# Moving the operands of every matmul to multiples of 128 and 1024 bytes in their partition

## The chip, the cores and the metric

The kernel runs on one core of a Trainium2 chip. The metric is the device time of one execution in microseconds (us), as the median of the runs. Five engines take part: TensorE (PE in the profile; its loads of stationary tiles are PEld), VectorE (DVE), ScalarE (ACT), GpSimd (POOL) and SyncE (SP), which here only issues DMAs.

## The reference

One decoder layer on x of 256 tokens by 1024 features, all in float32:

```python
h = rmsnorm(x, g_pre)
q_a, k_a, v_a, g_a, x_m, z_m = split(h @ w_in)      # w_in: 1024 x 6144
o_a = causal attention, 8 heads of 128, plus a bias by distance
y_a = o_a * silu(g_a)
x_c = silu(depthwise conv of width 4 over x_m)
q_m, k_m, v_m = block-diagonal 4x4 projections of x_c, x_c, x_m
h_m = mLSTM (4 heads of 256) with gates from q_m, k_m, v_m, then a LayerNorm per head
y_m = (h_m + skip * x_c) * silu(z_m)
out = x + rmsnorm(concat(y_a, y_m) @ w_out, g_post)  # w_out: 2048 x 1024
```

## The kernel before, in words

**Precision and tiles.** The two large projections use the type fp32r. Each float32 operand is split into a hi part, rounded to fp32r, and a lo part, the rest; a product is hi*hi + hi*lo + lo*hi, so three matmuls stand for one. The input projection goes through 24 chunks of 256 columns of `w_in` (8 tiles of 128 rows by 256 columns, a `raw` tile of 1 MB); the output projection goes through 8 chunks of `w_out`, 1 MB each. SyncE's queue brings the chunks four ahead (L76), ScalarE rounds them into `hi` (L90) and VectorE subtracts to get `lo` (L100). There are three buffers each of raw, hi and lo.

**The input projection.** `hhi` and `hlo` hold the transposed input, scaled by `g_pre`, 8 tiles of 128x256. `project` (L512) handles half a chunk in one call: 24 matmuls with 256 moving columns, stationary a 128x128 piece of the weights and moving a piece of `hhi` or `hlo`; for the v chunks stationary and moving change places. The first two chunks go through `project_quarter` (L522), quarter by quarter as the data comes in.

**The order.** It is written out by hand (manual schedule). The list `chunks` says which chunk is next: four of x_m ("m"), four of the gate g, then q, k and v of each pair of attention heads, the z chunks before the last pair. Two slots make a chunk. After each chunk `evacuate` scales its PSUM bank and starts a generator (`conv`, `gates`, `mlstm_head`, `attend`, `gate_a`, `gate_z`); in each slot `run_side` issues the next step of every generator that is due ahead of the half chunk's matmuls. Small matmuls thus stand between the halves: `vps` (L279) and `qps` (L286) of the block-diagonal projections, `gp` (L297) and `gif` (L304) of the gates, transposes `cp` (L331), `ht` (L389) and `atp` (L426) with `ident`, scores `sp` (L341, L344) and `as` (L406, L407), and the products `nps` (L362), `ao` (L437, L438). Those on float32 tiles are done by the chip in two passes, so they stand twice in the counts of the trace; transposes and fp32r matmuls stand once. A factor from the RMS norm comes in late: `rp` (L180) spreads it over the partitions with one matmul, which needs the sums over `xtok`, a 1 MB load.

**The output projection.** `multiply_out` (L591) takes five pieces of the output (three of 512 columns, two of 256) through 16 row tiles, again three matmuls each: stationary `yah`/`yal` (attention) or `ymh`/`yml` (mLSTM), moving the hi and lo tiles of `w_out`. `finish` and `store` scale with the second norm and write out.

**Where tiles lie.** A pool takes a stretch of every partition and its tiles lie one behind the other in the order of their first request, each rounded up to 32 bytes; a pool with n buffers holds n of each. The pools `cst` (constants), `wts` (raw, hi, lo), `wrk` (work tiles and many tiny ones of 4 to 48 bytes) and `big` follow each other from byte 16512 on. Since tiny tiles and tiles of odd widths lie between the large ones (`sm` of 816 bytes, `nhalf`, `rcol`, `amn`, `st`, `xt` of 8224 bytes, `xma` of 6216), the large ones begin at whatever multiple of 32 comes next:

| tile | start, mod 1024 | mod 128 |
|---|---|---|
| raw, hi, lo (all nine) | 704 | 64 |
| hhi, hlo, xc, yml, bias | 480 | 96 |
| ident, gsplit and apt | 960 | 64 |
| yal | 576 | 64 |
| yah (eight) | 992 | 96 |
| ymh, v1h | 608 | 96 |
| v1l | 672 | 32 |
| q, k and v of a pair (qkv) | 480 or 736 | 96 |
| qp | 448 | 64 |

Inside a tile the pieces step by 512 or 1024 bytes, except in `v1h` and `v1l` (258 columns a head, 1032 bytes) and in `xma` and `xmb` (259 columns, 1036 bytes).

Of the kernel before, what the change touches and what calls it, by code (L numbers as in the profile page):

```python
# [10 lines left out]
F32 = mybir.dt.float32  # L11
F32R = mybir.dt.float32r
# [5 lines left out]
P = 128  # L18
D = 1024
S = 256  # L20
KT = D // P
AH = 8
MH = 4
EH = 256
# [20 lines left out]
def hybrid_layer(ctx, tc, x, xg, small, wide, bias_t, g_post, w_in, w_out, out):  # L45
    nc = tc.nc
    pe, act, dve, pool = nc.tensor, nc.scalar, nc.vector, nc.gpsimd

    cst = ctx.enter_context(tc.tile_pool(name="cst", bufs=1))
# [4 lines left out]
    ctx.enter_context(tc.manual_schedule())  # L54

# [49 lines left out]
    big = ctx.enter_context(tc.tile_pool(name="big", bufs=1))  # L105


    xt = big.tile([P, 8 + KT * S], F32, tag="qp", name="xt")
    sm = cst.tile([P, NSMALL], F32, name="sm")
# [17 lines left out]
    ident = cst.tile([P, P], F32, name="ident")  # L127
    pool.affine_select(ident, ones[:, 0:P], pattern=[[1, P]], compare_op=OP.is_equal, fill=0.0,
                       base=0, channel_multiplier=-1)
    nhalf = cst.tile([P, 2], F32, name="nhalf")  # L130
    pool.memset(nhalf, -0.5)
    wake = wrk.tile([P, 2], F32, name="wake")
# [24 lines left out]
    rcol = cst.tile([P, 2], F32, name="rcol")  # L157
    rbc = cst.tile([P, S], F32, name="rbc")

    def rms_sums():  # L160
        junk = xc.rearrange("p a b -> p (a b)")
        ss = wrk.tile([P, 2], F32, name="ss")
        for t in range(2):
            act.activation(junk[:, t * D:(t + 1) * D], xtok[:, t, :], AF.Square,  # L164
                           accum_out=ss[:, t:t + 1])
        return ss
# [11 lines left out]
    def rms_spread(dg):  # L178
# [9 lines left out]
    xms = (big.tile([P, 6, S + 3], F32, tag="xm", name="xma"),  # L188
           big.tile([P, 2, S + 3], F32, tag="xmv", name="xmb"))
# [5 lines left out]
    v1h = big.tile([P, 2, MH, EH + 2], F32R, tag="v1", name="v1h")  # L195
    v1l = big.tile([P, 2, MH, EH + 2], F32R, name="v1l")

    tmp = big.tile([P, 1280], F32, tag="ym1", name="tmp")
    tmpv = big.tile([P, 576], F32, tag="ym1v", name="tmpv")
# [15 lines left out]
    def setup():  # L215
# [3 lines left out]
        aqk = cst.tile([P, 8, 4], F32, name="aqk")  # L219
# [35 lines left out]
    gc = cst.tile([P, 4, MH], F32, name="gc")  # L255
# [78 lines left out]
    def mlstm_head(h):  # L334
# [18 lines left out]
        st = wrk.tile([P, 2, 6], F32, name="st")  # L353
        mv = wrk.tile([P, 2, 2], F32, name="mv")
        den = wrk.tile([P, 2], F32, name="den")
# [13 lines left out]
        al = wrk.tile([P, 2], F32, name="al")  # L369
# [5 lines left out]
        be = wrk.tile([P, 2], F32, name="be")  # L375
# [25 lines left out]
    def attend(h):  # L401
# [7 lines left out]
        mn = wrk.tile([P, 2], F32, name="amn")  # L409
        rs = wrk.tile([P, 2], F32, name="ars")  # L410
# [206 lines left out]
    ss = [wrk.tile([P, 8], F32, name="oss") for _ in range(2)]  # L617
    ms = [wrk.tile([P, 1], F32, name="oms") for _ in range(2)]
# [46 lines left out]
NSMALL = 204  # L665
# [69 lines left out]
```

## Time and profile before

| | us |
|---|---|
| median of 3 runs | 234.74 |
| lowest and highest | 231.98, 234.98 |
| the profiled execution's own time | 233.72 |
| its span, first to last instruction | 232.0 |
| TensorE busy in it | 221.0 |
| VectorE busy | 159.7 |
| ScalarE busy | 128.4 |

The profile is one execution. Busy times of TensorE come from matmuls that are pipelined, with modelled ends, so they overlap: one matmul of 256 columns has a busy time of some 280 ns while the next one starts some 117 ns after it. The distance from start to start, or a stretch divided by its matmuls, is the cost of one. The chain of waits is followed back from the last instruction and lists the pieces that set the end.

### The profile page before, as it was taken

What the parts mean: (1) busy time and instruction counts of PE and PEld (TensorE: products, weight loads), DVE (VectorE), ACT (ScalarE), POOL (GpSimd) and SP (SyncE); (2) the same over time, 40 slices, a digit from 0 to 9 for tenths busy, and PEclk for the clock granted to TensorE, in tenths of its full rate; (3) what the DMA queues carried; (4) which work ended last, traced back from release to release, by engine and by line L of the source; (5) the groups of instructions that cost most, each with busy time, mean ns of one, the idle gap of its engine ahead of it and who ended that gap; (6) DMA issues with size and microseconds to landing.
All of it is one profiled execution on the core that took longest, in us unless ns stands there. A gap on an engine that the chain in (4) does not pass through costs nothing.

```text
span 232.0 us, 4213 instructions
## 1 busy us (share of the span) xinstructions
PE 221.0 (95%) x1684; PEld 210.2 (91%) x1684; DVE 159.7 (69%) x316; ACT 128.4 (55%) x227; POOL 29.8 (13%) x49
## 2 busy tenths in 40 slices
PE   7897899999999999999999999999999999999980
PEld 7797899999889999999999999999999888888870
DVE  1754999999924957646588988987884654474163
ACT  4755735777646946336565564896564714533220
POOL 2000395000000131000043364000000000000000
PEclk9999999999999999999999999999999999999996
DMA  6999783455541377454022523544544644550022
GB/s 157 326 419 418 292 319 164 181 185 181 184 181 37 148 253 249 179 181 168 16 72 113 181 58 127 181 184 181 181 185 181 209 175 161 228 225 3 0 90 92
DMA packets 8164, 40.95 MB, mean 177 GB/s; under 512 B 908, under 2 KB 1424, under 8 KB 4176
## 3 DMA queue, kind: packets, MB, share of 16 engines
q1 hardware_dynamic: 7744, 39.70, 47.0%
q0 software_dynamic: 256, 0.79, 1.2%
q8 instruction: 13, 0.21, 0.3%
q10 hardware_dynamic: 144, 0.20, 0.2%
q14 instruction: 7, 0.06, 0.1%
HBM read 39.63 MB, written 1.05 MB: 175 GB/s over the span
## 4 chain that ended last, share of the span: by engine, by line
PE 84%; DMA 7%; issue 2%; ACT 1%; SPq 1%; DVE 1%; POOL 1%; POOLq 0%; DVEq 0%
PE proj L512 52%; PE acc L591 17%; DMA xtok<-in_x_dram 4%; DMA xt<-in_xg_dram 3%; PE nps L362 2%; PE vps L279 2%; PE as L406 1%; PE qps L286 1%; PE sp L341 1%; PE ao L437 1%; PE atp L426 1%; ACT xc L164 1%; PE gp L297 1%; PE sp L344 1%; PE ao L438 1%
## 5 line engine op out<-in xcount | busy, mean ns | idle before, releaser
L100 DVE TENSOR_TENSOR lo<-raw,hi 128x1024 fp32r<-128x1024 f32 (+1 forms) x68 | 78.4, 1165 | 6.2 <-ACT hi L90 6.2
L90 ACT CAST hi<-raw 128x1024 fp32r<-128x1024 f32 (+1 forms) x68 | 66.3, 996 | 15.5 <-issue 7.7
L512 PE MATMUL proj<-hhi,hi 128*128 128x256 f32 x288 | 42.0, 288 | 0.0
L512 PE MATMUL proj<-hhi,lo 128*128 128x256 f32 x288 | 39.5, 279 | 0.0
L512 PE MATMUL proj<-hlo,hi 128*128 128x256 f32 x288 | 39.5, 279 | 0.0
L512 PEld LDWEIGHTS proj<-hhi,hi 128*128 128x128 f32 x288 | 36.6, 188 | 1.1 <-issue 0.8
L512 PEld LDWEIGHTS proj<-hlo,hi 128*128 128x128 f32 x288 | 36.2, 188 | 0.0
L512 PEld LDWEIGHTS proj<-hhi,lo 128*128 128x128 f32 x288 | 36.2, 188 | 0.0
L591 PE MATMUL acc<-hi,ymh 128*128 128x512 f32 (+1 forms) x40 | 14.3, 358 | 0.0
L591 PE MATMUL acc<-lo,yah 128*128 128x512 f32 (+1 forms) x40 | 14.0, 350 | 0.0
L591 PE MATMUL acc<-hi,yml 128*128 128x512 f32 (+1 forms) x40 | 14.0, 350 | 0.0
L591 PE MATMUL acc<-hi,yah 128*128 128x512 f32 (+1 forms) x40 | 14.0, 350 | 0.0
L591 PE MATMUL acc<-lo,ymh 128*128 128x512 f32 (+1 forms) x40 | 14.0, 350 | 0.0
L591 PE MATMUL acc<-hi,yal 128*128 128x512 f32 (+1 forms) x40 | 13.9, 348 | 0.0
L610 POOL TENSOR_TENSOR oms<-oms,nhalf 128x1 f32<-128x1 f32 x2 | 1.1, 568 | 81.2 <-DVE oms L607 81.2
L429 ACT CAST apt<-atp 128x256 fp32r<-128x256 f32 x8 | 3.0, 371 | 15.1 <-PE atp L426 15.1
L384 POOL TENSOR_SCALAR qp<-xc,sm 128x256 f32<-128x256 f32 x8 | 9.6, 1205 | 0.0
L603 ACT ACTIVATE sq<-acc 128x512 f32<-128x512 f32 (+1 forms) x5 | 2.6, 512 | 12.3 <-PE acc L591 12.3
L273 ACT ACTIVATE xc<-cv,sm 128x256 f32<-128x256 f32 x8 | 4.1, 511 | 9.5 <-DVE cv L269 9.5
L512 PE MATMUL proj<-hi,hhi 128*128 128x256 f32 x64 | 9.3, 287 | 0.0
L269 DVE SCALAR_TENSOR_TENSOR cv<-xma,sm,cv 128x256 f32<-128x256 f32 x18 | 8.8, 487 | 0.4
L512 PE MATMUL proj<-hi,hlo 128*128 128x256 f32 x64 | 8.9, 281 | 0.0
(165 smaller groups left out, 371.7 us busy)
## 6 DMA issues: line engine op xcount, KB each, us to landing
raw<-in_w_in_dram SPq DMA_DIRECT2D x22, 1024.0 KB, 4.9
raw<-in_w_out_dram SPq DMA_DIRECT2D x8, 1024.0 KB, 4.8
raw<-in_w_in_dram SPq DMA_DIRECT2D x8, 256.0 KB, 6.2
xtok<-in_x_dram SPq DMA_DIRECT2D x1, 1024.0 KB, 10.4
bias<-in_bias_dram SPq DMA_DIRECT2D x1, 1024.0 KB, 7.0
xr<-in_x_dram SPq DMA_DIRECT2D x1, 1024.0 KB, 7.2
xt<-in_xg_dram SPq DMA_DIRECT2D x3, 256.0 KB, 5.9
dl<-mdr POOLq DMA_DIRECT2D x1, 512.0 KB, 4.8
```

What stands on the lines that cost most here:

```text
L90: act.copy(his[n][:, sl], raws[n][:, sl])
L100: dve.tensor_tensor(los[n][:, sl], raws[n][:, sl], his[n][:, sl].bitcast(F32), OP.subtract)
L164: act.activation(junk[:, t * D:(t + 1) * D], xtok[:, t, :], AF.Square, accum_out=ss[:, t:t + 1])
L269: dve.scalar_tensor_tensor(cv[:, i], xm(f)[:, j:j + S], cols[:, 8 + 8 * j + f:9 + 8 * j + f], cv[:, i], op0=OP.mult, op1=OP.add)
L273: act.activation(xc[:, f, :], cv[:, i], AF.Silu, bias=cols[:, 40 + f:41 + f])
L279: pe.matmul(vps[:, t, i * P:(i + 1) * P], xm(f)[:, 3 + t * P:3 + (t + 1) * P], bdv[:, f, :], start=True, stop=True)
L362: pe.matmul(n[:, 0:EH + 2], gh[:, a, o:o + P], b[:, s, h, :], start=i == 0 and s == 0, stop=i == 2 and s == t)
L384: pool.tensor_scalar(u[:, f, :], xc[:, f, :], cols[:, 56 + f:57 + f], None, op0=OP.mult)
L429: act.copy(pt[:, 0], tp[:, 0:S])
L512: pe.matmul(ps[:, m, :], a, b, start=first and j == ks[0] and k == 0, stop=last and j == ks[-1] and k == KT - 1)
L591: pe.matmul(acc[p][:, 0:w], yt[:, t * P:(t + 1) * P], wt[:, i * D + c:i * D + c + w], start=j == 0 and i == 0 and q == 0, stop=j == 7 and ...
L603: act.activation(sq[:, 0:w], a, AF.Square, accum_out=ss[t][:, p:p + 1])
```

## The change

No instruction is added, dropped or moved; tiles get other places.

- `whole` allocates a tile whose row is rounded up to a multiple of `unit` elements (256, so 1024 bytes, unless given; 32, so 128 bytes, where given) and gives back the wanted shape as a slice of it. It is used for `xt`, `sm`, `ident`, `xms`, `v1h`, `v1l` and `tmpv`.
- `bit` does the same for tiny tiles in units of 32 bytes, and takes them from a pool of their own, `tny`, with two buffers, that comes after `big`. `nhalf`, `wake`, `rcol`, `ss`, `aqk`, `gc`, `st`, `mv`, `den`, `al`, `be`, `amn`, `ars`, `oss` and `oms` go there.
- `pad`, 896 bytes that nothing uses, moves the first pool's tiles from 16512 to 17408, a multiple of 1024.

Afterwards `hhi`, `hlo`, raw, hi and lo tiles, `ident`, `yal` and the work tiles begin at multiples of 1024 bytes, and the tiles of `big` at multiples of 128. The steps inside `v1h`, `v1l`, `xma` and `xmb` are as before.

```diff
--- before.py
+++ after.py
@@ -52,6 +52,18 @@
     psm = ctx.enter_context(tc.tile_pool(name="psm", bufs=8, space=PSUM))
     drm = ctx.enter_context(tc.tile_pool(name="drm", bufs=1, space=DRAM))
     ctx.enter_context(tc.manual_schedule())
+    cst.tile([P, 224], F32, name="pad")
+
+    def whole(pool, shape, dtype, unit=256, **kw):
+
+        n = math.prod(shape[1:])
+        t = pool.tile([P, -(-n // unit) * unit], dtype, **kw)[:, 0:n]
+        names = "abcd"[:len(shape) - 1]
+        dims = {k: v for k, v in zip(names[1:], shape[2:])}
+        return t.rearrange("p (%s) -> p %s" % (" ".join(names), " ".join(names)), **dims)
+
+    def bit(shape, name):
+        return whole(tny, shape, F32, unit=8, name=name)
 
     def bank(name):
         return psm.tile([P, 512], F32, tag="bank", name=name)
@@ -103,10 +115,11 @@
 
 
     big = ctx.enter_context(tc.tile_pool(name="big", bufs=1))
-
-
-    xt = big.tile([P, 8 + KT * S], F32, tag="qp", name="xt")
-    sm = cst.tile([P, NSMALL], F32, name="sm")
+    tny = ctx.enter_context(tc.tile_pool(name="tny", bufs=2))
+
+
+    xt = whole(big, [P, 8 + KT * S], F32, unit=32, tag="qp", name="xt")
+    sm = whole(cst, [P, NSMALL], F32, name="sm")
     cols, wb, blk, sel, bif = (sm[:, o:o + n] for o, n in SMALL)
     wb = wb.rearrange("p (i t o) -> p i t o", i=3, o=4)
     bif = bif[0:MH]
@@ -124,12 +137,12 @@
 
     ones = cst.tile([P, 256], F32, name="ones")
     dve.memset(ones, 1.0)
-    ident = cst.tile([P, P], F32, name="ident")
+    ident = whole(cst, [P, P], F32, name="ident")
     pool.affine_select(ident, ones[:, 0:P], pattern=[[1, P]], compare_op=OP.is_equal, fill=0.0,
                        base=0, channel_multiplier=-1)
-    nhalf = cst.tile([P, 2], F32, name="nhalf")
+    nhalf = bit([P, 2], "nhalf")
     pool.memset(nhalf, -0.5)
-    wake = wrk.tile([P, 2], F32, name="wake")
+    wake = bit([P, 2], "wake")
     act.activation(wake, ones[:, 0:2], AF.Silu)
 
     def stay_awake(n):
@@ -154,12 +167,12 @@
         split_hi(0, q, parts=4)
         split_lo(0, q, parts=4)
 
-    rcol = cst.tile([P, 2], F32, name="rcol")
+    rcol = bit([P, 2], "rcol")
     rbc = cst.tile([P, S], F32, name="rbc")
 
     def rms_sums():
         junk = xc.rearrange("p a b -> p (a b)")
-        ss = wrk.tile([P, 2], F32, name="ss")
+        ss = bit([P, 2], "ss")
         for t in range(2):
             act.activation(junk[:, t * D:(t + 1) * D], xtok[:, t, :], AF.Square,
                            accum_out=ss[:, t:t + 1])
@@ -185,18 +198,18 @@
     bd = big.tile([P, 16, P], F32R, tag="ym0", name="bd").bitcast(F32)
     bda, bdv = bd[:, 0:8, :], bd[:, 8:16, :]
     bias = None
-    xms = (big.tile([P, 6, S + 3], F32, tag="xm", name="xma"),
-           big.tile([P, 2, S + 3], F32, tag="xmv", name="xmb"))
+    xms = (whole(big, [P, 6, S + 3], F32, unit=32, tag="xm", name="xma"),
+           whole(big, [P, 2, S + 3], F32, unit=32, tag="xmv", name="xmb"))
 
     def xm(f, n=1):
         t, f = (xms[0], f) if f < 6 else (xms[1], f - 6)
         return t[:, f, :] if n == 1 else t[:, f:f + n, :]
 
-    v1h = big.tile([P, 2, MH, EH + 2], F32R, tag="v1", name="v1h")
-    v1l = big.tile([P, 2, MH, EH + 2], F32R, name="v1l")
+    v1h = whole(big, [P, 2, MH, EH + 2], F32R, unit=32, tag="v1", name="v1h")
+    v1l = whole(big, [P, 2, MH, EH + 2], F32R, unit=32, name="v1l")
 
     tmp = big.tile([P, 1280], F32, tag="ym1", name="tmp")
-    tmpv = big.tile([P, 576], F32, tag="ym1v", name="tmpv")
+    tmpv = whole(big, [P, 576], F32, unit=32, tag="ym1v", name="tmpv")
 
     wkr = tmp[:, 0:128]
     wifr = tmp[:, 128:896].rearrange("p (i n) -> p i n", i=3)
@@ -216,7 +229,7 @@
         qk = half_kb("qk", 128).rearrange("p (t j o) -> p t j o", j=4, o=4)
         dve.tensor_tensor(qk, wb[:, 0].unsqueeze(2).to_broadcast([P, 8, 4, 4]),
                           wkr.rearrange("p (t j o) -> p t j o", j=4, o=4), OP.mult)
-        aqk = cst.tile([P, 8, 4], F32, name="aqk")
+        aqk = bit([P, 8, 4], "aqk")
         dve.tensor_reduce(aqk, qk, axis=mybir.AxisListType.X, op=OP.add)
         dve.tensor_scalar(aqk, aqk, EH ** -0.5, None, op0=OP.mult)
         for t in range(8):
@@ -252,7 +265,7 @@
 
     ymh = yml = None
     dl = cst.tile([P, MH, 384], F32, name="dl")
-    gc = cst.tile([P, 4, MH], F32, name="gc")
+    gc = bit([P, 4, MH], "gc")
     qp = u = None
 
     def conv(c, ps):
@@ -350,9 +363,9 @@
         yield 1
         dve.tensor_tensor(gh[:, 1], g, gh[:, 0].bitcast(F32), OP.subtract)
         yield 1
-        st = wrk.tile([P, 2, 6], F32, name="st")
-        mv = wrk.tile([P, 2, 2], F32, name="mv")
-        den = wrk.tile([P, 2], F32, name="den")
+        st = bit([P, 2, 6], "st")
+        mv = bit([P, 2, 2], "mv")
+        den = bit([P, 2], "den")
         nps = []
         for t in range(2):
             n = bank("nps")
@@ -366,13 +379,13 @@
             dve.bn_stats(st[:, t, :], nps[t][:, 0:EH])
             dve.tensor_copy(den[:, t:t + 1], nps[t][:, EH:EH + 1])
             dve.bn_aggr(mv[:, t, :], st[:, t, :])
-        al = wrk.tile([P, 2], F32, name="al")
+        al = bit([P, 2], "al")
         dve.scalar_tensor_tensor(al, den, -1.0, gc[:, 2:4, h], op0=OP.mult, op1=OP.max)
         dve.tensor_tensor(al, al, den, OP.max)
         dve.scalar_tensor_tensor(al, al, LN_EPS, al, op0=OP.mult, op1=OP.mult)
         dve.tensor_tensor(al, al, mv[:, :, 1], OP.add)
         pool.tensor_tensor(al, al, nhalf, OP.pow)
-        be = wrk.tile([P, 2], F32, name="be")
+        be = bit([P, 2], "be")
         dve.scalar_tensor_tensor(be, mv[:, :, 0], -1.0, al, op0=OP.mult, op1=OP.mult)
         yield 1
         hn = wrk.tile([P, 2, EH], F32, name="hn", bufs=1)
@@ -406,8 +419,8 @@
         pe.matmul(sp[:, 0:S], qt[:, i, P:], kt[:, i, :], start=True, stop=True)
         pe.matmul(sp[:, S:384], qt[:, i, 0:P], kt[:, i, 0:P], start=True, stop=True)
         e = half_kb("ae", 384)
-        mn = wrk.tile([P, 2], F32, name="amn")
-        rs = wrk.tile([P, 2], F32, name="ars")
+        mn = bit([P, 2], "amn")
+        rs = bit([P, 2], "ars")
         parts = ((0, 0, S), (1, S, 384))
         for a, o, z in parts:
             dve.tensor_tensor_reduce(e[:, o:z], sp[:, o:z], bias[:, h, S - (z - o):], -1.0, 3.0e38,
@@ -614,8 +627,8 @@
         dve.scalar_tensor_tensor(o, o, ms[t], xr[:, t, c:c + w], op0=OP.mult, op1=OP.add)
         queue.dma_start(dram(out, t * P * D + c, [[D, P], [1, w]]), o)
 
-    ss = [wrk.tile([P, 8], F32, name="oss") for _ in range(2)]
-    ms = [wrk.tile([P, 1], F32, name="oms") for _ in range(2)]
+    ss = [bit([P, 8], "oss") for _ in range(2)]
+    ms = [bit([P, 1], "oms") for _ in range(2)]
     for j in range(8):
         for m in range(2):
             while done:
```

## Rows read from the trace of the kernel before

**Rows 1.** The page: busy us (share of the span) and instructions by engine; granted TensorE clock in 40 slices.

```profile
PE 221.0 (95%) x1684; PEld 210.2 (91%) x1684; DVE 159.7 (69%) x316; ACT 128.4 (55%) x227; POOL 29.8 (13%) x49
...
PEclk9999999999999999999999999999999999999996
```

**Rows 2.** The page: the chain that ended last, shares by engine, then by line.

```profile
PE 84%; DMA 7%; issue 2%; ACT 1%; SPq 1%; DVE 1%; POOL 1%; POOLq 0%; DVEq 0%
PE proj L512 52%; PE acc L591 17%; DMA xtok<-in_x_dram 4%; DMA xt<-in_xg_dram 3%; PE nps L362 2%; PE vps L279 2%; PE as L406 1%; PE qps L286 1%; PE sp L341 1%; PE ao L437 1%; PE atp L426 1%; ACT xc L164 1%; PE gp L297 1%; PE sp L344 1%; PE ao L438 1%
```

**Rows 3.** Waits of TensorE over the span: us in total, times, longest us.

```profile
PE rp L180 <- DVE dg L175: 2.5, 1, 2.5
...
PE proj L522 <- ACT hi L90: 0.6, 2, 0.4
```

**Rows 4.** Timeline of L591 near its end: start us, us, engine, line, operation, tiles, form, count.

```profile
218.91 0.39 PE L591 MATMUL acc<-hi,yah 128*128 128x512 f32 x1
...
221.91 0.39 PE L591 MATMUL acc<-hi,yal 128*128 128x512 f32 x1
...
223.20 0.28 PE L591 MATMUL acc<-hi,yal 128*128 128x256 f32 x1
...
224.97 0.28 PE L591 MATMUL acc<-hi,yal 128*128 128x256 f32 x1
225.09 0.28 PE L591 MATMUL acc<-lo,yah 128*128 128x256 f32 x1
```

**Rows 5.** Chain in order of time, L512: start us, us, engine, tile, line, count.

```profile
24.93 14.01 PE proj L512 x120
...
47.23 2.80 PE proj L512 x24
...
96.32 2.84 PE proj L512 x24
...
160.45 16.88 PE proj L512 x144
```

**Rows 6.** Chain in order of time: plain f32 matmuls and transposes.

```profile
46.34 0.89 PE vps L279 x8
...
50.03 0.86 PE qps L286 x4
...
108.76 0.22 PE as L407 x2
...
121.06 0.44 PE ht L389 x4
```

**Rows 7.** Chain in order of time: the nps matmuls of heads 0 to 3.

```profile
111.79 1.08 PE nps L362 x9
...
121.50 1.08 PE nps L362 x9
...
130.33 1.09 PE nps L362 x9
...
139.03 1.08 PE nps L362 x9
```

**Rows 8.** Windows of 5 us: busy us (count) of PE, PEld, DVE, ACT, POOL; PEclk, DMA share, GB/s.

```profile
25.00:30.00 5.00, 5.00 (x45) 5.00 (x44) 4.93 (x10) 3.42 (x5) 2.40 (x4) 1.00 0.73 272
...
35.00:40.00 5.00, 5.00 (x45) 5.00 (x45) 4.86 (x9) 2.38 (x5) 3.22 (x5) 1.00 0.43 180
...
55.00:60.00 5.00, 5.00 (x42) 4.89 (x41) 4.89 (x9) 3.16 (x8) 0.00 (x0) 1.00 0.62 216
```

**Rows 9.** Timeline of VectorE and TensorE near 41 us.

```profile
40.36 1.21 DVE L100 TENSOR_TENSOR lo<-raw,hi 128x1024 fp32r<-128x1024 f32 x1
...
41.56 1.11 PE L512 MATMUL proj<-hhi,lo 128*128 128x256 f32 x8
```

**Rows 10.** Timeline of ScalarE and TensorE near 79 us.

```profile
78.95 0.42 ACT L320 ACTIVATE fb<-fb 4x256 f32<-4x256 f32 x1
...
80.18 0.26 PE L331 MATMUL cp<-ident,fb 4*128 4x4 f32 x2
```


## The prediction

> **What bounds the kernel now.** I read the page first. TensorE is busy 221.0 of 232.0 us, the next engine (VectorE) 69% [rows 1]. Busy time of pipelined matmuls overlaps, so it proves little by itself; the chain that ended last does: 84% of it is TensorE, 52% the projection matmuls of L512 and 17% the output projection of L591 [rows 2]. Third, the waits: apart from 0.6 us inside the first chunk, TensorE waits for another engine only once after its wake-up, 2.5 us before `rp` [rows 3]. That wait hangs on a DMA (`xtok`), so what TensorE saves ahead of it is lost again, and what it saves from there (24.9 us) to its last matmul at 225.09 us [rows 4] shortens the run one for one, unless another engine comes late. [...] So the question is the spacing of matmuls in that stretch.
>
> **The spacing.** One half chunk of L512 is 24 matmuls of 256 columns (fp32r) and takes 2.80 us, 116.7 ns each; six z and other halves in a row take 16.88 us for 144, 117.2 each; a v chunk, where the operands are swapped, takes 2.84, 118.3 each [rows 5]. In L591, 13 matmuls of 512 columns take 221.91 - 218.91 = 3.00 us, 231 each, and 15 of 256 columns 224.97 - 223.20 = 1.77, 118 each [rows 4].
>
> Is that the speed of the array? Rows of plain f32 on the same engine say no. Such a matmul is two passes, each with its own load of a 128x128 stationary tile: 256 columns take 0.86/4 = 215 ns a pass, 128 columns 0.22/2 = 110, and the transposes of 128 columns 0.44/4 = 110 [rows 6]. So a plain column costs (215 - 110)/128 = 0.82 ns, and 5 ns come on top of a pass. An fp32r column costs (231 - 117.5)/256 = 0.443 by L591, where half of 0.82 is 0.41. With that half, 256 fp32r columns should take the 110 ns of 128 plain ones, and 512 should take the 215. The excess is then 6.7 ns per projection matmul, 16 per matmul of 512 and 8 per one of 256 in L591. This excess is all that a change of addresses alone can win in the matmuls.
>
> [...]
>
> **The change part by part.** Instructions, their order, their queues, waits and sizes stay: the diff only gives tiles other shapes to be allocated in and slices them back, puts the tiny tiles into a pool of their own with as many buffers as before or more, and adds `pad`, which nothing writes or reads. So nothing is removed, no wait is added and no DMA is added or moved. The price of all of that is nothing; no cover is needed, since no instruction comes in. What changes is where operands start: hi, lo and raw tiles go from 704 to 0 (mod 1024), hhi and hlo from 480 to 0, everything else that a matmul touches from 0, 32, 64 or 96 to 0 (mod 128), apart from the steps inside `xm` and v1. ScalarE, VectorE and the DMAs read and write the same tiles; they end off the path, and I take no gain or loss there.
>
> *Does the start matter?* No matmul of L512 or L591 shows an aligned pair, so I bound it. Low end, nothing: the `nps` matmuls of the four heads have moving tiles that start at 96+32s+8h bytes (mod 128), so head 0 has two of nine at an exact multiple of 128 and heads 1 and 3 have none even at a multiple of 16, and they take 1.08, 1.08, 1.09 and 1.08 us [rows 7]. So the start of the moving tile alone does nothing. High end, the whole excess: 1032 x 6.7 = 6.9 us in L512 (so many of its 1056 matmuls stand in the pieces of the chain; the other 24 run before the wait and don't count), in L591 144 x 16 + 96 x 8 = 3.1 us, in `nps` and `ao` some 60 x 8 = 0.5 us, together 10.5. Below nothing: see the last rival.
>
> Between these ends I go by the nearest rows with a full load and a stream of equal length. Where both operands start at the same place mod 128 (L407 both at 96, the transposes both at 64) the pass takes 110; where they differ (the vps of L279) 0.89/8 = 111 [rows 6]. And the swap of operands alone, 64 under 96 against 96 under 64, makes 2.84 of 2.80 [rows 5]. Both differences are small, but they say that the two streams into the array, the matmul's and the next load's, feel each other's addresses. After the change they agree everywhere, and in L512 mod 512. I therefore take the full 6.9 us for L512, half of the 3.1 for L591 (only 128 there: 1.5), nothing for the rest: 8.4 us.
>
> *What is late next.* VectorE is busy 4.93, 4.86 and 4.89 of 5 us in three stretches between 25 and 60 us [rows 8]; it has nothing to spare while it prepares the lo tiles. The tightest is the second half of lo5: written at 40.36 + 1.21 = 41.57, first read by the fifth matmul of the group that begins at 41.56, so at 42.03, a margin of 0.46 us [rows 9]. By then TensorE would be 144 x 6.7 = 0.96 us ahead, so it waits 0.5. The gates are next: `fb` is ready at 79.37 and read at 80.18, a margin of 0.8 us [rows 10], of which TensorE takes about 108 x 6.7 = 0.7 back between 67 and 80 us, and the chain has VectorE steps in it: 0.2. If VectorE holds the whole stretch to 60 us, some 266 matmuls gain nothing there and the give-back is 1.8 us in place of 0.5.
>
> The sum: 8.4 - 0.5 - 0.2 = 7.7 us off the profiled execution's 233.72 (its span of 232.0 and 1.7 around it), 226.0. The median of the runs, 234.74, lies 1.0 above that execution, so 227.0 against the median. Its own range is 224 to 230.
>
> **The rivals.** *Nothing or next to nothing.* The excess belongs to fp32r, whose column may just cost 0.443. For: [rows 7], where even a start off any 16-byte mark costs nothing; and the spacing of 116.7 is the same for both halves of a chunk, though the stationary tile starts 512 bytes apart. Against: the 0.82 of plain columns, and the v chunks. With the differences that rows do show, 1.6 ns (118.3 against 116.7) on all 1272 matmuls, it wins 2.0 us at most: 232.7 to 234.7.
>
> [...]
>
> *All of it and more.* Both projections go to 110 and 215, `nps` and `ao` too: 10.5 - 1.0 given back, 224.2 and, if nothing is given back, 224.2 - 1.0 = 223.2. For: the arithmetic of half a plain column. Against: `nps` keeps its 8-byte steps, and L591 gets only 128.
>
> *Slower.* The load of the next tile and the matmul's stream start together, and now at the same place mod 512: if the streams disturb each other where they meet in the same part of a line, agreement is the worst case and not the best. Place: L512. Nothing in the trace shows it; the price I take is the excess a second time, 6.7 x 1032 = 6.9 and 1.5 in L591: 243. It decides from 4.5 ns per projection matmul on (4.7 us, 2%). For: the addresses are felt. Against: L407 and the transposes agree and are the fastest of their kind [rows 6].
>
> **How the numbers follow.** Forecast 0.40, nothing or little 0.40, all of it 0.10, slower 0.10. The first two are as good as equal; the rows with agreeing operands decide for the forecast. A measurement of this kernel can tell about 2% (4.7 us, so 230.0 and 239.4) from no change: faster is the forecast and the third, 0.50; within 2% the second, 0.40; slower 0.10. The range must hold both of the large cases: 223 to 237; it leaves out most of the slower case and the edge of the third.
>
> **What would show it.** Right: halves of L512 at 2.62 to 2.65 us, v chunks the same as the others, L591 at some 222 ns, a wait of about 0.5 us of TensorE for lo L100 near 41 us, everything before 24 us as it was. Nothing: 2.80 again, v at 2.80 or 2.84. Slower: halves of 2.9 us and more. Wrong in another way: other idle times of TensorE, or DMA landings that differ from before.

## The result, and the profile after

| | before | after |
|---|---|---|
| median of 20 runs each, us | 234.48 | 235.30 |
| lowest and highest | 231.98, 236.19 | 234.48, 237.70 |
| the profiled execution, and its span | 233.72, 232.0 | 235.19, 233.5 |

The ratio is 1.007 with a 95% interval of 1.0047 to 1.0093. The forecast was a gain of 7.7 us; what came is a small loss. It is far within 2%, yet the interval leaves out 1.

TensorE is busier, and the granted clock is at 0.9 of full speed or more in all 40 slices but the last, as before [rows 1].

```profile
PE 223.7 (96%) x1684; PEld 212.9 (91%) x1684; DVE 159.6 (68%) x316; ACT 128.2 (55%) x227; POOL 29.8 (13%) x49
...
PEclk9999999999999999999999999999999999999997
```

In the chain in order of time, L525 is what L512 was and L604 what L591 was. A half of 24 matmuls takes 2.87 to 2.88 us where it took 2.80, a v half (the one at 96.52) 2.87 where it took 2.84, and the 144 in a row 17.28 where they took 16.88 [rows 5]. The f32 passes and `nps` are what they were [rows 6, 7].

```profile
23.09 0.70 PE rp L193 x2
23.79 14.38 PE proj L525 x120
...
45.67 0.89 PE vps L292 x8
46.56 2.88 PE proj L525 x24
...
96.52 2.87 PE proj L525 x24
...
107.35 0.86 PE sp L354 x4
108.21 0.44 PE sp L357 x4
...
109.09 0.22 PE as L420 x2
...
112.19 1.09 PE nps L375 x9
...
121.57 0.44 PE ht L402 x4
...
161.51 17.28 PE proj L525 x144
```

The output projection has not moved: nine steps of 512 columns take 221.80 - 219.70 = 2.10 us, 233 ns each, against 231 to 232 [rows 4].

```profile
219.70 0.40 PE L604 MATMUL acc<-hi,yah 128*128 128x512 f32 x1
...
221.80 0.40 PE L604 MATMUL acc<-hi,yah 128*128 128x512 f32 x1
```

From start to start, averaged over the trace's single matmuls, the projections went from 116.9 to 119.8 ns, and the v chunks from 118.2 to 119.7. 840 times 2.9 and 192 times 1.5 are 2.7 us. The span is only 1.5 us longer because in this execution `xtok` landed earlier (at 19.24 us, not 20.39), so that `rp` starts at 23.09 us instead of 24.24 and TensorE waits 1.5 us for it instead of 2.5 [rows 3].

```profile
PE rp L193 <- DVE dg L188: 1.5, 1, 1.5
...
PE proj L535 <- ACT hi L102: 0.4, 2, 0.2
```

The start of `rp` differs from execution to execution. So I compare the stretch from there to the end, span less start of `rp`: 232.0 - 24.24 = 207.8 us before, 233.5 - 23.09 = 210.4 after. That is 2.6 us, and so is the sum over the projections to within 0.1. Below, this stretch is called the tail. Two questions follow: why did the projections get slower, and why does the median show 0.8 us where the tail shows 2.6?

### The profile page after: what moved, and what is told of

Same layout as the page of the kernel before. It is cut to its first block, busy times and chain, and to the rows that moved or that the text cites. A ratio compares the mean times of both kernels' runs of the same rounds, so it can differ in the third digit from the quotient of the medians.

```text
span 233.5 us, 4214 instructions
## 1 busy us (share of the span) xinstructions
PE 223.7 (96%) x1684; PEld 212.9 (91%) x1684; DVE 159.6 (68%) x316; ACT 128.2 (55%) x227; POOL 29.8 (13%) x49
## 4 chain that ended last, share of the span: by engine, by line
PE 85%; DMA 7%; issue 2%; ACT 1%; SPq 1%; DVE 1%; POOL 1%; POOLq 0%; DVEq 0%
PE proj L525 53%; PE acc L604 17%; DMA xtok<-in_x_dram 4%; DMA xt<-in_xg_dram 3%; PE nps L375 2%; PE vps L292 2%; PE as L419 1%; PE qps L299 1%; PE sp L354 1%; PE ao L450 1%; PE atp L439 1%; ACT xc L177 1%; PE gp L310 1%; PE sp L357 1%; PE as L420 1%
## 5 line engine op out<-in xcount | busy, mean ns | idle before, releaser
L525 PE MATMUL proj<-hhi,hi 128*128 128x256 f32 x288 | 42.7, 291 | 0.0
L525 PE MATMUL proj<-hlo,hi 128*128 128x256 f32 x288 | 40.4, 283 | 0.0
L525 PE MATMUL proj<-hhi,lo 128*128 128x256 f32 x288 | 40.4, 283 | 0.0
L525 PEld LDWEIGHTS proj<-hhi,hi 128*128 128x128 f32 x288 | 37.2, 191 | 1.1 <-issue 0.8
L525 PEld LDWEIGHTS proj<-hhi,lo 128*128 128x128 f32 x288 | 37.2, 192 | 0.0
L525 PEld LDWEIGHTS proj<-hlo,hi 128*128 128x128 f32 x288 | 37.1, 192 | 0.0
L604 PE MATMUL acc<-hi,ymh 128*128 128x512 f32 (+1 forms) x40 | 14.3, 358 | 0.0
L604 PE MATMUL acc<-hi,yah 128*128 128x512 f32 (+1 forms) x40 | 14.0, 351 | 0.0
L604 PE MATMUL acc<-hi,yal 128*128 128x512 f32 (+1 forms) x40 | 14.0, 350 | 0.0
L604 PE MATMUL acc<-hi,yml 128*128 128x512 f32 (+1 forms) x40 | 14.0, 350 | 0.0
L604 PE MATMUL acc<-lo,ymh 128*128 128x512 f32 (+1 forms) x40 | 14.0, 350 | 0.0
L604 PE MATMUL acc<-lo,yah 128*128 128x512 f32 (+1 forms) x40 | 14.0, 350 | 0.0
L525 PE MATMUL proj<-hi,hhi 128*128 128x256 f32 x64 | 9.4, 289 | 0.0
L525 PE MATMUL proj<-hi,hlo 128*128 128x256 f32 x64 | 9.0, 283 | 0.0
```

The lines of the kernel that those rows point to most:

```text
L525: pe.matmul(ps[:, m, :], a, b, start=first and j == ks[0] and k == 0, stop=last and j == ks[-1] and k == KT - 1)
L604: pe.matmul(acc[p][:, 0:w], yt[:, t * P:(t + 1) * P], wt[:, i * D + c:i * D + c + w], start=j == 0 and i == 0 and q == 0, stop=j == 7 and ...
```

## The experiments

"Distance" is from here on the start of the moving operand less the start of the stationary one, in bytes. In the kernel before it is 480 - 704 = -224 in the projections, which is 32 modulo 256 (224 in the v chunks); afterwards it is 0.

**The projections alone.** In the kernel before, three tiles that nothing uses put `hhi`, `hlo`, raw, hi and lo at multiples of 1024; everything else that a matmul touches stays off the multiples of 128.

```diff
+    wrk.tile([P, 16], F32, name="padc", bufs=1)
...
+    cst.tile([P, 136], F32, name="pad")
     hhi = cst.tile([P, KT, S], F32R, name="hhi")
...
+        cst.tile([P, 200], F32, name="padb")
```

> The kernel before, with hhi, hlo, raw, hi and lo alone moved to multiples of 1024 bytes by pads; every other tile that a matmul touches keeps its start mod 128, apart from yal (64 to 96). If the loss sits in the projections: halves of L512 at 2.87 to 2.88 us, v chunks too, and 1.006 to 1.012 of the kernel before. If it sits in the other tiles: halves at 2.80 and 1.000.

Measured: 235.69 us, ratio 1.0086 (1.0053 to 1.0119); 119.8 ns a projection matmul, 17.27 us for the 144, a tail of 233.8 - 23.36 = 210.4. The whole loss is in the projections' operands.

**Start or distance.** The changed kernel with its first pad 480 bytes longer: all starts are 96 modulo 128, all distances stay.

```diff
-    cst.tile([P, 224], F32, name="pad")
+    cst.tile([P, 344], F32, name="pad")
```

> The kernel after, with the first pad 480 bytes longer, so that every large tile begins 480 bytes later (96 mod 128) and all distances between tiles stay. Theory R (relation of the two operands): halves of the projection stay at 2.87 us and the time at 1.007 of the kernel before. Theory S (start mod 128 by itself): halves go back to 2.80 us, 1.000.

Measured: 236.23 us, ratio 1.0106 (1.0054 to 1.0159), again 119.8 ns. Two of the six runs, the profiled one among them, had a mean granted clock under 0.99 (more on that below), so here the spacing decides and not the time. It is not where the tiles start that costs, but that the two operands of a matmul start at the same place.

**The distance by itself.** Behind the changed kernel's own work, groups of 24 matmuls from two tiles, the moving one at offset a, the stationary one at b, all of them behind one another.

```diff
+        for j in range(n):
+            k = 256 * (j % 6) * step
+            pe.matmul(pb[0:load, 0:cols], his[NALL - 2][:, b // 4 + k:b // 4 + k + load],
+                      los[NALL - 1][:, a // 4 + k:a // 4 + k + cols], start=True, stop=True)
```

> The kernel after, with 33 groups of 24 extra fp32r matmuls behind the last store, which write a PSUM bank that nobody reads (the output is as before; the time is longer by these groups). In each group the moving operand starts at byte a and the stationary one at byte b of a 1024-byte-aligned tile, and both step by 1024 bytes as in the projections. Theory R (relation): the spacing depends on a - b; 119.8 ns at a = b whatever a is, 116.7 at (480, 704), 118.2 at (704, 480). Theory S (start): it depends on where an operand starts in its 128 bytes; 119.8 at (0, 0) and (128, 0), and 116 to 118 at (32, 32), (64, 64) and (96, 96). Theory L (load): the excess over 110 ns comes from the load that runs beside the stream; with a load of 32 columns the spacing falls to 109 or 110, and 512 columns with it to 215. Theory I (intrinsic): an fp32r column costs 0.445 ns; with a load of 32 columns the spacing stays at 115 or more.

The timeline gives a group's start; the next group's start less it, by 24, is the cost of one. `pac` is at distance 32, `pad` at 64, `pae` at 96; `paw` and `pax` are at 0 and 32 with a load of 32 columns instead of 128; `pay` and `paz` are at 0 and 32 with 512 moving columns. `pas` has the starts of the kernel before, moving at 480 and stationary at 704, and `pau` the reverse, as in its v chunks.

```profile
232.78 2.97 PE L668 MATMUL pac<-lo,hi 128*128 128x256 f32 x24
235.58 2.89 PE L668 MATMUL pad<-lo,hi 128*128 128x256 f32 x24
238.30 3.04 PE L668 MATMUL pae<-lo,hi 128*128 128x256 f32 x24
241.18 3.01 PE L668 MATMUL paf<-lo,hi 128*128 128x256 f32 x24
...
278.19 2.98 PE L668 MATMUL pas<-lo,hi 128*128 128x256 f32 x24
281.00 2.96 PE L668 MATMUL pat<-lo,hi 128*128 128x256 f32 x24
283.80 3.00 PE L668 MATMUL pau<-lo,hi 128*128 128x256 f32 x24
286.63 2.88 PE L668 MATMUL pav<-lo,hi 128*64 128x256 f32 x24
289.36 2.88 PE L668 MATMUL paw<-lo,hi 128*32 128x256 f32 x24
292.08 2.98 PE L668 MATMUL pax<-lo,hi 128*32 128x256 f32 x24
294.89 5.62 PE L668 MATMUL pay<-lo,hi 128*128 128x512 f32 x24
300.36 5.77 PE L668 MATMUL paz<-lo,hi 128*128 128x512 f32 x24
305.96 5.76 PE L668 MATMUL pba<-lo,hi 128*128 128x512 f32 x24
```

Distance 32 costs 2.80/24 = 116.7 ns, 64 costs 113.3, 96 costs 120, and 0 settles at 120 like 96, also with both starts at 32, 64 or 96. The starts of the kernel before settle at 116.7 (`pas`) and 118.2 (`pau`), where that kernel has 116.9 and 118.2 on average. So theory R holds, and S falls. With the short load, 0 costs 113.3: the load of the next tile takes part, and a full one at distance 0 adds 6.7 ns. Theories L and I both miss, since 113.3 lies between their figures. Nor is a short load always out of the way: with it, distance 32 stays at 117.5. At 512 columns 0 is the fast case: it costs 5.47/24 = 228 (227 once settled), 32 costs 233.

A second round of the same probe, with the step j % 4 and more distances:

> The kernel after with 46 groups of 24 extra fp32r matmuls behind the last store, as in the first probe (the time is longer by them; the output stays). Moving starts at byte a, stationary at b. First part, loads of 32 columns, so that the load is out of the stream's way: theory M (the stream has a grid of its own) expects 113.4 ns at a = 0, 64, 128 and 117 or so at 16, 32, 48, 80, 96. Second part, loads of 128 columns: theory R64 (the two streams stay apart when the moving operand starts 64 bytes off the stationary one, mod 128) expects 113.4 at (64, 0), (64, 512), (192, 0), (320, 0), (576, 512), (128, 64), (0, 64), (0, 192) and 120 at (0, 512); theory A (it hangs on the start of the moving operand alone, 64 mod 128, with the stationary at 0) expects 113.4 at (64, 0), (64, 128), (64, 256), (192, 512) and 118 or more at (128, 64), (96, 32) and (0, 64). Third part: the same four pairs after a plain f32 matmul, to see whether the state at the start decides; if it does not, 120, 113.4, 117.8, 116.7. Fourth part, 512 columns: 226.7 at (0, 0) and (64, 0), 233 at (32, 0).

Distance 0 is at 120 again, but 64 is now at 117.8 and -64 at 113.3, the reverse of the first round. Loads of 32 columns settle at 113.3 at distances 0, 16, 48, 64 and 128, and at 116 to 118 at 32, 80 and 96, so theory M holds in part. Starts or distances off the multiples of 16 are no better (both operands 4 bytes on, first round: 122; a distance of 72: 121.5). So a distance can have more than one repeating pattern (64: 113.3 and 117.8 ns), and within a group of 24 the stream stays in the one it has fallen into.

**64 bytes apart.** The changed kernel with `hhi` and `hlo` 64 bytes past a multiple of 1024.

```diff
-    cst.tile([P, 224], F32, name="pad")
+    cst.tile([P, 160], F32, name="pad")
...
+    sm = whole(cst, [P, NSMALL], F32, unit=8, name="sm")
...
+    ident = whole(cst, [P, P], F32, unit=8, name="ident")
...
     hlo = cst.tile([P, KT, S], F32R, name="hlo")
+    cst.tile([P, 240], F32, name="padb")
```

> The kernel after, with hhi and hlo 64 bytes further (64 mod 1024) and hi, lo and raw at 0 as before, by a shorter first pad and a pad behind hlo; sm and ident lie closer. If the first probe's pair (64, 0) holds in the kernel: halves of the projections that stream hhi and hlo at 24 x 113.4 = 2.72 us, v chunks, where hhi is stationary, at 24 x 117.8 = 2.83; 840 x 3.5 + 192 x 0.4 = 3.0 us less than before, 0.987 of it. If the pair was an accident of the probe's start: halves at 2.80 to 2.88 and 1.000 to 1.010.

Measured: 233.29 us, ratio 0.9973 (0.9935 to 1.0012), 116.9 ns on average outside the v chunks, so the 0.987 of the first case did not come. In its chain each half sits in one of two patterns, 2.83 us (117.9 ns) or 2.74 (114), and keeps it until other matmuls come between:

```profile
24.42 0.70 PE rp L194 x2
...
96.50 2.83 PE proj L526 x24
100.64 2.74 PE proj L526 x24
104.27 2.83 PE proj L526 x24
```

**Which distance has only a fast pattern?** Eight distances, each entered after f32 matmuls of eight widths, 16 matmuls a group; and both kernels once more.

> The kernel after with 64 groups of 16 extra fp32r matmuls behind the last store (output as before, time longer): eight distances of the moving operand from the stationary one, 0 to 112 bytes in steps of 16, and for each eight entries, two plain f32 matmuls of 24 to 128 columns ahead of the group. Theory K (one spacing for each distance): all eight entries of a distance settle at the same spacing, 120 at 0. Theory P (several repeating patterns for a distance, the entry picks one and the stream keeps it): 120 at 0 whatever the entry; at 64 both 113.4 and 117.8; at 32 116.7 and 117.8.

> The kernel before once more, for a second profile. If the first load's landing (rp at 24.2 us) and the spacings (117 with some halves at 117.8) belong to the kernel, they come again; if they vary from execution to execution, rp lies elsewhere between 23 and 24.5 us and other halves have 2.83.

> The kernel after once more, for a second profile. Halves of the projections at 2.87 to 2.88 in every chunk again; rp at 23.1 us if the earlier landing of xtok belongs to the aligned tiles, between 23 and 24.5 if it varies by itself.

| distance | settled, ns | groups |
|---|---|---|
| 0 | 120.0 | 8 of 8 |
| 16 | 118.6; 116.6; 113.4 | 5; 2; 1 |
| 32 | 116.6 to 116.8; 117.5 | 7; 1 |
| 48 | 118.4 | 8 of 8 |
| 64 | 117.6 to 117.9 | 8 of 8 |
| 80 | 120.0; 118.4 | 7; 1 |
| 96 | 119.4 to 120.2 | 8 of 8 |
| 112 | 113.4, after some eight at 116 to 121 | 8 of 8 |

Only 0, 48, 64, 96 and 112 gave one answer here, and only 112 a fast one. The two kernels gave 232.56 and 236.11 us in single runs, with tails of 230.8 - 23.15 = 207.7 and 234.4 - 23.99 = 210.4 us: the tails repeat within 0.1 us, the start of `rp` does not.

**112 modulo 128 in the kernel, and 512 columns in a probe.** `hhi` and `hlo` begin 28 floats into wider tiles; hi and lo tiles are widened as well (8320 bytes each) so that the v chunks can begin 24 floats in.

```diff
+    def off(pool, o, **kw):
+        return pool.tile([P, 2080], F32R, **kw)[:, o:o + 2048]
...
+            his[n] = off(wts, voff(n), tag="hi", name="hi%d" % n)
...
+    hhi = off(cst, 28, name="hhi").rearrange("p (k n) -> p k n", n=S)
+    hlo = off(cst, 28, name="hlo").rearrange("p (k n) -> p k n", n=S)
```

> The changed kernel with the projections' moving operands 112 bytes past the stationary ones, modulo 128, everywhere (v chunks too). Theory (the distance decides, and 112 is the one that settled at 113.4 ns in all eight groups of the probe): each run of projection matmuls goes to 113.4 ns after some eight matmuls at about 118, a half of 24 takes 2.72 to 2.80 us where the changed kernel takes 2.87, the 144 in a row 16.4 us where it takes 17.3; 1032 matmuls by about 5 ns are 5 us less than the changed kernel, 2.5 less than before: a ratio of 0.985 to 0.992 to the kernel before. Rival (the pattern depends on what came before and is drawn anew after every transpose and copy): stretches at 117 to 120 stay, and the ratio is 0.997 or more.

> The changed kernel with, behind its own work, groups of 18 matmuls of 512 columns in the order that L591 uses, the distance from the stationary operand's start to the moving operand's start being 0, 16, 32, ... 112 bytes past a multiple of 128, each after matmuls of 128, 64 and 24 columns. Theory (the distance decides, as it does at 256 columns): the groups differ by distance, and one of them, 112 as at 256 columns or 0 as in the probe before, is at 227 ns a matmul while the others are at 231 to 234. Rival (at 512 columns the load lies beside so little of the stream that the distance does not matter): all groups within 1 ns of 233.

The kernel: 233.06 us, ratio 0.9963 (0.9932 to 0.9993), 117.5 ns on average, the 144 in 16.91 us, a tail of 230.1 - 22.43 = 207.7: a miss. Only some stretches were at 113.4. Since the wider tiles no longer step by a multiple of 1024, the distances were 112 in half of the matmuls and 240 in the other half, modulo 256; the ten groups of eight that came to 113.4 all stood at 112, though forty more at 112 did not get there. The probe at 512 columns: 227 at distance 0, 229 at 64, 231 to 233 at all others, whatever went ahead.

**Order, or other engines?** Groups of 42 matmuls in the order of the projections, first alone, then with five subtractions on VectorE and six copies on ScalarE beside each group.

> The changed kernel with groups of 42 matmuls of 256 columns in the projections' own order behind its work, moving minus stationary 0, 32, 64 and 112 bytes past a multiple of 128, three groups each, first alone and then beside a row of subtractions on VectorE and copies on ScalarE of 1024 columns. Theory A (the order of operands, not the company, keeps the kernel from 113.4 at distance 112): 112 stays at 116 to 118 alone as beside the others. Theory B (other engines' traffic to the same memory knocks the stream out of its pattern): 112 and one of the 64s are at 113 to 114 alone and at 116 to 118 beside them. Distance 0 is 120 in both, by either.

The second third of a group (14 matmuls), start to start of the next third: at distance 0 (`paa`) 1.68/14 = 120.0 ns, at 112 (`paj`) 1.59/14 = 113.6; beside the other engines (`pam`, `pav`) the same 1.68 and 1.59.

```profile
230.24 1.84 PE L683 MATMUL paa<-lo,hi 128*128 128x256 f32 x14
231.92 1.84 PE L683 MATMUL paa<-hi,lo 128*128 128x256 f32 x14
...
278.93 1.75 PE L683 MATMUL paj<-lo,hi 128*128 128x256 f32 x14
280.52 1.75 PE L683 MATMUL paj<-hi,lo 128*128 128x256 f32 x14
...
295.46 1.84 PE L683 MATMUL pam<-lo,hi 128*128 128x256 f32 x14
297.14 1.84 PE L683 MATMUL pam<-hi,lo 128*128 128x256 f32 x14
...
353.84 1.75 PE L683 MATMUL pav<-lo,hi 128*128 128x256 f32 x14
355.43 1.75 PE L683 MATMUL pav<-hi,lo 128*128 128x256 f32 x14
```

Neither theory stands: the order of the projections lets 112 settle, and VectorE and ScalarE do not disturb it. (Next to no DMA ran beside them, a share of 0.02 and 0.00 in two of the groups, so transfers are not tested.) What remained was 112 against 240.

**112 everywhere, and 240 everywhere.** `hhi` and `hlo` in one tile, so that they stay 8192 bytes apart, the hi and lo tiles at multiples of 1024 as in the changed kernel; pads in `big` put `yah`, `ymh` and `yml` at multiples of 512; four matmuls more ahead of `rp` (their reason stands below).

```diff
+    hh = cst.tile([P, 4128], F32R, name="hh")
+    hhi, hlo = (hh[:, o:o + 2048].rearrange("p (k n) -> p k n", n=S) for o in (28, 2076))
+    cst.tile([P, 224], F32, name="padb")
...
+    big.tile([P, 96], F32, name="padc")
     bd = big.tile([P, 16, P], F32R, tag="ym0", name="bd").bitcast(F32)
...
+    big.tile([P, 64], F32, name="padd")
     v1h = whole(big, [P, 2, MH, EH + 2], F32R, unit=32, tag="v1", name="v1h")
```

The second kernel differs by 32 floats: `(60, 2108)`, and a `padb` that much shorter.

> The changed kernel with hhi and hlo 112 bytes past a multiple of 1024 (hi and lo stay at multiples of it), all of L591's stationary operands at multiples of 512, and four matmuls of 128 columns ahead of rp. Theory (in the run with distance 112 modulo 128 the stretches at 112 modulo 256 went to 113.4 ns after three to five matmuls, those at 240 modulo 256 never did, and the two took turns within a half): with 112 everywhere the chunks m, q, k, a and z go to 113.4 ns after some ten matmuls, a half of 24 takes 2.72 to 2.77 us, the 512-column matmuls 227 to 228 ns: some 840 times 3 ns and 139 times 5 ns are 3.2 us less than before, 229.5 to 231 us, a ratio of 0.980 to 0.988. Rival (in the kernel something else breaks the pattern, so that 117 stays): halves of 2.80 us, 231.5 to 232.5, ratio 0.991 to 0.995.

> The same with hhi and hlo 240 bytes past a multiple of 1024, which is 112 modulo 128 too. Theory (modulo 256 counts, 240 does not settle): halves at 2.81 to 2.83 us, 117 to 118 ns a matmul, some 2 to 3 us more than with 112. Rival (modulo 128 is all that counts): the same as with 112, within 0.02 us a half.

With 112: 231.33 us, ratio 0.9876 (0.9829 to 0.9922), a tail of 229.5 - 23.66 = 205.8 us. The ratio flatters it: seven of the eleven runs of before beside it had a mean clock under 0.99, and one of its own six. The tail is 1.9 us shorter than before's: the projections outside the v chunks take 2.1 us less and L591 0.6 less, but the v chunks 0.35 more and the `gp` matmuls 0.46 more. With 240: a single run of 232.12 us, a tail of 230.4 - 22.92 = 207.5, so 1.6 us more than with 112 where 2 to 3 were expected. The chain with 112, where the half at 95.23 is a v half (there the distance is -112, 144 modulo 256, and costs 120 ns):

```profile
23.66 0.70 PE rp L196 x2
...
95.23 2.88 PE proj L530 x24
...
112.41 2.74 PE proj L530 x24
117.11 2.79 PE proj L530 x24
...
158.80 16.66 PE proj L530 x144
...
200.78 16.58 PE acc L609 x84
```

And with 240:

```profile
22.92 0.70 PE rp L196 x2
...
112.39 2.81 PE proj L530 x24
...
159.33 17.01 PE proj L530 x144
```

Apart from the v chunks, the first averages 114.2 ns and the second 117.2: 128 bytes, a whole multiple of 128, make 3.0 ns a matmul. The distance counts modulo 256 and not modulo 128. The first probe agrees: there distances 256 and 512 settle at 120 like 0, and 128 at 118.8.

**The clock in the wait for `rp`.** The profile of the run with the longer pad above had the clock fall during that wait. Windows of it (busy us of PE, PEld, DVE, ACT, POOL; then the granted clock, DMA share, GB/s):

```profile
22.00:23.00 1.00, 0.00 (x0) 0.00 (x0) 0.17 (x1) 0.60 (x3) 0.07 (x1) 1.00 1.01 419
23.00:24.00 1.00, 0.00 (x0) 0.00 (x0) 0.33 (x2) 1.00 (x2) 0.63 (x1) 0.88 1.00 412
24.00:25.00 1.00, 0.80 (x3) 0.71 (x3) 1.00 (x2) 0.96 (x2) 0.00 (x0) 0.50 0.96 401
25.00:26.00 1.00, 1.00 (x5) 0.91 (x5) 1.00 (x2) 0.00 (x0) 0.00 (x0) 0.50 0.71 295
26.00:27.00 1.00, 1.00 (x7) 1.00 (x6) 0.96 (x4) 0.43 (x1) 0.00 (x0) 0.50 0.18 74
```

TensorE stands idle, the clock goes to 0.50 of full speed and stays there for three microseconds of matmuls; the tail is 236.0 - 24.20 = 211.8 us, 1.4 more than the 210.4 of the same spacing. The mean clock of that execution is 0.984 where the others have 0.99. Do the runs of before mix the two? Seven matmuls of 128 columns fill most of the wait, in both kernels:

```diff
         rp = bank("rp")
+        for _ in range(7):
+            pe.matmul(rp[:, S:384], ones[:, 0:P], ones[:, 0:P], start=True, stop=True)
```

A third kernel has them on top of the 64 bytes from above, and `yah` at multiples of 512 (128 bytes that nothing uses ahead of it).

```diff
     gs, yah = {}, {}
+    big.tile([P, 32], F32, name="pady")
```

> The kernel before with seven matmuls of 128 columns more ahead of rp, so that TensorE works through most of its wait for dg. Theory (the runs of the kernel before fall into two groups because in some of them the clock drops while TensorE waits for rp: 10 runs at a mean clock of 0.99 have a median of 232.9, 7 at 0.984 have 235.0): no run is left at 0.984, all lie at 232 to 234, the median is 1 to 1.5 us below that of before (ratio 0.994 to 0.997). Rival (the clock drop has another place or cause): both groups stay, and the ratio is 1.00 or, with a filler that delays rp, up to 1.003.

> The changed kernel with the same seven matmuls ahead of rp. Theory (19 of its 20 runs were at 0.994 already, and its projections start every 119.8 ns): 235 to 236 as without them, and 1.009 to 1.013 of the kernel before with the seven, since the 2.9 us of the trace are then no longer hidden in before's spread. Rival (the median's smaller loss of 0.8 us is the true one): 1.003 of it.

> The changed kernel with hhi and hlo 64 bytes past a multiple of 1024, the seven matmuls ahead of rp, and yah at multiples of 1024 (of 512 for its second half) instead of 896 past one. Theory (distance 64 leaves matmuls at 113.4 or 117.8 ns; the clock stays up; the 512-column matmuls go from 233 to 227 ns where both operands start at a multiple of 512): 231.5 to 232.5 us, ratio 0.988 to 0.993 to before, the last 84 matmuls in 16.3 to 16.5 us instead of 16.9. Rival for the last part (multiples of 512 do not do it): they stay at 16.8 to 16.9.

Of the 29 runs of before beside them, 19 have a mean clock of 0.99 or more and a median of 232.6 us, and 10 have 0.986 or less and 235.2. With the seven matmuls no run of the 12 is at the lower clock: 232.51 to 233.68, median 233.16, ratio 0.9976 (0.994 to 1.0012). Nor is any of the 12 runs of either other kernel with the seven; with the four of the section above one run in six was (0.983). The low group is gone, as the theory said, but the median is not lower: fewer runs of before were low this time (10 of 29, where the theory went by 7 of 17), and the median with the filler is 0.6 us above that of the 19. The changed kernel with them: 235.78, ratio 1.0098 (1.0065 to 1.0131) to before, and 235.78/233.16 = 1.011 to before with the same filler. That is 2.6 us, the difference of the tails.

The third: 232.25 us, ratio 0.9929 (0.9893 to 0.9965), and 232.25/233.16 = 0.996 to before with the same filler. Its last 84 matmuls take 16.57 us, a little more than expected. Those of 512 columns among them take (220.65 - 218.61)/9 = 227 ns where the changed kernel's take 233:

```profile
218.61 0.39 PE L608 MATMUL acc<-hi,yah 128*128 128x512 f32 x1
...
220.65 0.39 PE L608 MATMUL acc<-hi,yah 128*128 128x512 f32 x1
```

## Why the prediction failed, by its steps

**What held.** TensorE bounds the kernel, and a change of spacing goes through to the end one for one: 2.7 us over the projections, 2.6 in the tail. No instruction, wait or transfer of the change costs anything: with the projections' operands alone moved the tail is 210.4 us as well. Starts by themselves do nothing: with all of them 480 bytes on, the spacing stays at 119.8 ns. But [rows 7], from which the prediction took that the start of the moving tile alone does nothing, did not carry over to the projections: there a moving tile 128 bytes further on cost 3.0 ns a matmul. The two streams, a matmul's columns and the next tile's load, do feel each other's addresses: with the same load, a matmul costs 113.3 to 120 ns in the first probe by the distance. Which case it is, was the error.

**The step that failed** is "Where both operands start at the same place mod 128 [...] the pass takes 110 [...] I therefore take the full 6.9 us for L512". It read 110 against 111 ns, and 2.84 against 2.80 us, as a gain from agreement, and carried it from plain f32 passes to fp32r. The f32 rows show the first reading to be empty. The operands of `sp` are the test: `xc` and `qp` begin at 96 and 64 modulo 128 before, and both at multiples of 128 after. Its passes take the same before as after (L354 and L357 above):

```profile
107.02 0.86 PE sp L341 x4
107.88 0.44 PE sp L344 x4
```

`vps` is no test, since its stationary pieces step by 1036 bytes and disagree with the moving ones after the change as well. Nor had L591 been without an aligned pair, as the prediction says: `yal` and the hi tiles both began at 64 modulo 128, and those matmuls of 512 columns averaged 230.3 ns against 230.2 for hi with `yah`. For 256 columns of fp32r, agreement is among the slowest cases: 120 ns at distance 0 in the kernel and in every probe with full loads. The kernel before stood at 32 and 224, at 116.9 and 118.2. So in place of the 6.9 us to be won, L512 lost 2.6 to 2.7.

**The term "excess" was too large as well.** It took 110 ns for the floor. The lowest spacing at which any group settled is 113.3 for 256 columns and 226.7 for 512 (the latter with a full load at distance 0; with a short load it was 231.7). 256 times the 0.443 ns per column of the prediction is 113.4. So no run here shows less than that, and by what the runs show the kernel before had 3.5 ns to win and not 6.7. The kernel with 112 everywhere took 2.6 of them outside the v chunks.

**"Half of the 3.1 for L591"** came out as nothing (232.4 to 233.0 ns on average). There agreement is the fast case, but agreement modulo 128 is not enough: after the change `yah` begins at 896 modulo 1024, 128 off the hi tiles modulo 256, and the second probe has 232 to 233 ns at 128. At multiples of 512 it gave 227. The probe and the kernel show this; why 512 columns want 0 and 256 columns want 112 is open.

**The give-back** of 0.7 us at lo5 and the gates had nothing to act on; TensorE got slower and no wait arose. Whether the 0.46 us that `gp` lost with 112 everywhere are of this kind is not shown.

**The rivals.** "Slower" had the place, the sign and the full load that disturbs the stream (120 ns at distance 0, 113.3 with a short one); that agreement alone is "the worst case" is not so, since 80 and 96 cost 120 as well. Its price was mis-sized: it took a second excess of 6.7 ns, where agreement added 2.9 to what the kernel before already paid, and by its own bound (4.5 ns) it stays within 2%. "Nothing or next to nothing" came nearest in time, and its 0.443 ns a column held, but the spacing did move, so it was near partly by luck. That the whole spacing belongs to fp32r does not agree with the probe, where a load of 128 columns in place of 32 adds 6.7 ns to the same stream at distance 0.

**Why the median shows so little.** The prediction compared one profiled execution with the median and did not ask what spreads the runs by 3 us. In the batches run beside the experiments, a third to two thirds of before's runs have a mean clock under 0.99, and their medians lie 1.2 to 2.6 us above the others'; 19 of the 20 runs after keep 0.99. Shown: the drop in one trace, that of the changed kernel with the longer pad, and that filling the wait of [rows 3] removes the low group and brings the full 2.6 us out in the medians. Not known: the clocks of the 20 runs of before in the table of the result. Not settled: why the changed kernel falls into it so seldom. The projections alone, at the same spacing, had 0 of 12 low runs and the longer pad 2 of 6; the kernels with 64 and 112 had 5 and 4 of 12. That TensorE comes to the wait later and waits less is only argued. Not tried: traces of before in the low group.

## What to carry to other kernels

Here the speed of back-to-back fp32r matmuls of 256 columns hung on where the moving operand starts relative to the stationary one (114.2 ns at 112 bytes, 117.2 at 240, 119.8 at 0), and rounding both up to the same multiple was among the worst choices: try a few distances with the real column count in a probe, then check them in the kernel. Two rows that differ by one per cent, of another data type, don't give the sign of such an effect. When runs spread, look at the granted clock of each and compare stretches that begin behind the jitter.

## What the runs showed of the hardware that was not expected

- In the probes, matmuls of 256 fp32r columns with loads of 128 settled into repeating patterns, of 113.4, 116.7, 117.8, 118.4 or 120 ns at most distances; at 64 two of them (113.4 and 117.8) held for whole groups. At 512 columns the best was 227 (both operands at the same place modulo 512) and the common one 231 to 233.
- A shift of 128 bytes, from 112 to 240, changes 114.2 into 117.2 ns in the kernel.
- Traffic of VectorE and ScalarE beside the matmuls left the pattern as it is (120.0 ns at distance 0 and 113.6 at 112, alone and beside).
- During an idle wait of 2.4 us the clock fell to 0.50 of full speed in one profiled execution; in others with waits of 2.5 and 2.8 us it did not.
